# A one-core encoder layer: written order for the mixer's projection units, pooling counts set up later, third T4 ahead and weights three ahead in the up projection

## The chip, the cores and the metric

One of the eight cores of a Trainium2 chip runs the whole program in one launch. The metric is the device time of an execution in microseconds (us). TensorE (PE) multiplies matrices, VectorE (DVE) and ScalarE (ACT) work on tiles of 128 partitions, GpSimd (POOL) does small element-wise work and issues some DMAs, SyncE (SP) issues most of the others.

## The reference

One layer over 2048 tokens of 1024 channels, all in float32:

```python
xn = rmsnorm(x, norm1_g)
u_pool, zq, zf, zi, zo, zg = split(xn @ w_in)
gates = sigmoid(zg + b_gate)
ya = pool_mixer(u_pool, pool_w, pool_scale) @ w_pa    # trailing means, windows 2/4/8/16
yb = hgrn2_mixer(zq, zf, zi, zo, lb, hgrn_norm_g) @ w_pb   # gated linear recurrence, 4 heads
x = x + (gates[0] * ya + gates[1] * yb) @ w_o
h = rmsnorm(x, norm2_g) @ w_up
val, gate = split(causal_depthwise_conv(h, width=3))
x = x + (silu(gate) * val) @ w_down
out = rmsnorm(x, final_g)
```

The pooling branch divides a window sum by a count, min(t, window); the count differs from the window only in the first tokens.

## The kernel before, in words

The 2048 tokens are four blocks of 512. Blocks are taken in pairs, so that the program has two passes, each with a mixer (input projection, pooling, recurrence, the two branch projections, output projection) and a feed-forward part (up projection, convolution and gate, down projection).

The large products use a two-by-two Strassen-like scheme with seven products instead of eight, named P1 to P7. One half of the operands is the pair of token blocks, the other a pair of output or weight quarters. The activations come in seven forms: B11, B21 and B22 are parts of the normalised input, T1 to T4 sums and differences of them (`FORM`). Each form has four tiles (k = 0 to 3). In tile names, x_f0 to x_f3 are B11 and x_f4 to x_f7 are B21 in the mixer; the feed-forward part's begin with m. Each operand is split into a high part, rounded by ACT (a cast), and a low part, the rest, by DVE; a product of one k is three matmuls (high by high, high by low, low by high), so a projection product has twelve.

A unit (`class Unit`) makes two output tiles for both token blocks from the products in the order P1, P6, P5, P7, P2, P4, P3 (`ORDER`). They gather in three PSUM banks: X takes P1 and then P2, Z takes P6, P7 and P4, V takes P5 and P3 (`BANK`). Between them values are taken out: e1 is ACT's copy of X after P1, u2 = e1 - Z after P6 (L1188), u3 = Z - e1 after P7 (L1192), and the four outputs after P2, P7, P4 and P3. So P2 may only write X after e1, P7 only write Z after u2, and P4 only after u3. The mixer has 14 units a pass in the order `PROJ`: fr are the units of the recurrence's forget gates and queries, gr the branch gates, ur the pooling channels. In traces a buffer's number is left out; in listings of an order fr_0 is the first fr unit. The io product (value and output gate of the recurrence, io_X, io_Y, io_Z, io_V) comes ahead of the units and has the same seven products with four banks each.

Weights come through `class Stream`: SP loads a raw tile, ACT and DVE split it (L230, L231) into one of six buffers, and conversion runs at most `LOOKAHEAD` = 4 products ahead of the product being issued. In the io product of the first pass some weights are sums, made by a DMA of POOL that adds to a raw tile (L165); there are eight of these, kept in the list `added`: four for P7's weights and four for P3's. DVE adds others (w8s to w11s, L384).

The code is written as one stream of matmuls (`mm`); every sixth one ticks a list of tasks, which write other engines' work: forms_b_task writes the forms T1 to T4 and B22, setup_task the masks of the recurrence and the reciprocal counts `inv`, hgrn_task the recurrence (its matmuls pl, pk, pv, po, pt stand between the units' on PE). A scheduler then sets the order on each engine by its own estimate of the time: an instruction that it holds to be ready may pass another. `behind(a, b)` forbids that for a and b: a stands behind b. In the up projection the second matmul of each product already stands behind the last matmul of the product before; in the mixer's units nothing holds the products in their order.

setup_task starts with P7 of io. Before, it begins with an iota on POOL, four minima with the windows on POOL (L611) and a reciprocal on DVE (L613), then eight masks and two more, in two scratch tiles in turn. The form T4 in the up projection is B21 - T2 on DVE (L861) and a split. Of its four tiles the third and fourth wait until the first u3 of a unit is written, and stand behind it.

Of the kernel before, what the change touches and what calls it, by code (L numbers as in the profile page):

```python
# [15 lines left out]
ALU = mybir.AluOpType  # L16
# [59 lines left out]
N_OPS = 6  # L76
# [5 lines left out]
def tile_trunk(  # L82
# [85 lines left out]
    class Stream:  # L168
        def __init__(self):
            self.raws = []  # L170
            self.ops = []
            self.n_raw = 0
            self.tiles = []
            self.next = 0
            self.done = 0
            self.pins = {}
            self.stop = None

        def raw(self, src, plus=None):
            r = Raw(src, plus)  # L180
# [57 lines left out]
        def advance(self, n):  # L238
            for _ in range(n):
                j = len(self.tiles)  # L240
                if j >= len(self.ops) or j == self.stop or j >= self.next + LOOKAHEAD or j - N_OPS >= self.done:
                    return
                self.convert()

# [13 lines left out]
    def behind(ins, other):  # L258

        tc.add_manual_dep(ins.ins, other.ins.name, mybir.DependencyInfo(  # L260
            mybir.DependencyClass.NoSync, mybir.DependencyReason.DATA), reason="behind")
# [338 lines left out]
    def setup_task():  # L600
        scratch = [hist.rearrange("p a b -> p (a b)")[:, :64], uhist.rearrange("p a b -> p (a b)")]

        def mask_of():
            scratch.reverse()
            return scratch[0]

        ins = pool.iota(inv[:, 3], pattern=[[1, 16]], base=1, channel_multiplier=0,
                  allow_small_or_imprecise_dtypes=True)
        behind(ins, last_root[0])
        for g, w in enumerate(WINDOWS):  # L610
            pool.tensor_scalar(inv[:, g], inv[:, 3], float(w), None, ALU.min)  # L611
        flat_inv = inv.rearrange("p a b -> p (a b)")
        dve.reciprocal(flat_inv, flat_inv)  # L613
        yield 1
        keys = [(h, h, 0, h) for h in (1, 2, 4, 16)]
        keys += [(8 * h + t, 2 * h, t * h, h) for h in (4, 16) for t in range(2)]
        for key, x, off, w in keys:
            nb = 64 // x
            mf = mask_of()
            behind(pool.memset(mf, 1.0), ins if len(masks) < 6 else added[3])  # L620
            v = mf.rearrange("p (b h) -> p b h", h=x)
            pool.affine_select(out=v, in_=v, pattern=[[-2 * x, nb], [0, x]],
                               compare_op=ALU.is_ge, fill=0.0, base=-off, channel_multiplier=1)
            pool.affine_select(out=v, in_=v, pattern=[[2 * x, nb], [0, x]],
                               compare_op=ALU.is_ge, fill=0.0, base=off + w - 1,
                               channel_multiplier=-1)
            m8 = const.tile([P, 64], U8, tag=f"m{key}", name=f"m{key}")
            yield 2
            pool.tensor_copy(m8, mf)
            masks[key] = m8.rearrange("p (b h) -> p b h", h=x)  # L630
        for t in range(2):
            mf = mask_of()
            behind(pool.memset(mf, 0.0), added[3])
            pool.affine_select(out=mf, in_=mf, compare_op=ALU.not_equal, fill=1.0, base=-t,
                               pattern=[[-2, 64]], channel_multiplier=1)
            m8 = const.tile([P, 64], U8, tag=f"md{t}", name=f"md{t}")
            yield 2
            pool.tensor_copy(m8, mf)
            masks[-1 - t] = m8.unsqueeze(1)
        pool.memset(hist, 0.0)  # L640
        pool.memset(uhist, 0.0)
        for h in range(HEADS):
            pool.memset(state[h, 0], 0.0)

# [146 lines left out]
    def forms_b_task(src, gain, forms, full, after, go, early):  # L791
# [24 lines left out]
        for k in range(4):  # L816
            while len(full["B11"]) <= k:
                yield 4
            p12 = turned(k)
            p22 = turned(k + 4)  # L820
            t = slot(f"{name}b{k}")
            act.activation(t, p22, AF.Copy, scale=negs[:, gain + k + 4 : gain + k + 5])
            b22.append(t)
            t1.append(minus("t1", k, p12, full["B11"][k]))
            t2 = minus("t2", k, p22, t1[k], k + 4)
            if src[0] == "m":
                t = slot(f"{name}t3{k}")
                pool.tensor_tensor(t, full["B11"][k], t2, ALU.subtract)
                t3.append(t)
            elif not early:  # L830
                t3.append(minus("t3", k, p12, b22[k], op=ALU.add))
            forms["T2"].append(split(t2, f"{name}T2{k}"))
            full["T2"].append(t2)
            yield 1
        for k in range(4):
            forms["T1"].append(split(t1[k], f"{name}T1{k}"))
            yield 2 if src[0] == "m" else 5
# [17 lines left out]
        for k in range(4):  # L855
            while len(full["B21"]) <= k:
                yield 4
            t4 = slot(f"{name}t4{k}")
            while src[0] == "m" and k > 1 and not forms.get("u3"):
                yield 1  # L860
            ins = dve.tensor_tensor(t4, full["B21"][k], full["T2"][k], ALU.subtract)  # L861
            if src[0] == "m" and k > 1:
                behind(ins, forms["u3"][0])
            while early and k and len(forms.get("u3", ())) < 4:
                yield 1
            if early and k > 1:
                behind(ins, forms["u3"][3])
            forms["T4"].append(split(t4, f"{name}T4{k}"))
            if early and k == 1:
                behind(last_split[0][1], forms["u3"][3])  # L870
            if early and k:
                stream.pins[20 + k] = last_split[0]
                while len(stream.tiles) <= 20 + k:
                    stream.convert()
                stream.stop = 21 + k if k < 3 else 25
                forms["low"] = stream.low
            if src[0] == "x" and not early:
                forms["B22"].append(split(b22[k], f"{name}B22{k}"))
            yield 1
        while len(forms["B22"]) < 4:  # L880
# [4 lines left out]
            if early:  # L885
# [7 lines left out]
                            stream.convert()  # L893
                stream.stop = 26 + k if k < 2 else None
            yield 1

    x2d = {}

# [254 lines left out]
    class Unit:  # L1153
# [10 lines left out]
        def multiply(self, p, forms, late):  # L1164
# [8 lines left out]
            for k in range(4):  # L1173
                wh, wl = w[:, 0, k * P : (k + 1) * P], w[:, 1, k * P : (k + 1) * P]
                xh, xl = xs[k]
                mm(ps, wh, xh, start=p in FIRST and k == 0, stop=False, skip_group_check=True)
                if k == 0 and self.key == "up":
                    behind(count[1], before)
                mm(ps, wh, xl, start=False, stop=False, skip_group_check=True)
                mm(ps, wl, xh, start=False, stop=k == 3, skip_group_check=True)  # L1180
# [687 lines left out]
```

## Time and profile before

| | |
|---|---|
| median of 3 runs | 2548.97 us |
| lowest and highest | 2546.82 and 2556.62 us |
| profiled execution | 2549.41 us, its span 2547.7 us |
| mean granted PE clock | 0.997 |
| first mixer with its start | 0 to about 640 us |
| first feed-forward part | about 640 to 1275 us |
| second mixer, second feed-forward part | about 1275 to 1890 us, 1890 us to the end |

A timeline row gives the start and the length in us, the engine, the line, the operation, the tile written and those read, sizes, count, and in brackets the idle time ahead of it with what ended it. A row of a window gives the busy time of each engine with the number of instructions, then the PE clock (1.00 is full), the share of DMA engines in use and GB/s. PE's ends are modelled.

### The profile page before, as it was taken

Reading aid. Unit: us, or ns where it says so; the run is one execution under the profiler, and the core shown is the slowest. Engines: PE = TensorE matmul, PEld = TensorE weight load, DVE = VectorE, ACT = ScalarE, POOL = GpSimd, SP = SyncE. Lnnn points to the kernel's source line nnn. Section 1 sums busy time; section 2 is a strip of 40 time slices with the busy share of each in tenths; the row PEclk is TensorE's granted clock in tenths of the full one; section 3 lists DMA queues with packets and bytes.
Section 4 is the critical chain, followed back from the end, with each engine's and each line's share of the span. In section 5 each row is a group of like instructions: output and inputs, shape, how many; then the busy total and the mean of one; then the engine's idle time right before and its main releaser. Section 6 shows DMA issues by size and latency. Waiting matters only on the chain.

```text
span 2547.7 us, 35661 instructions
## 1 busy us (share of the span) xinstructions
PE 2515.0 (99%) x11508; PEld 2059.6 (81%) x11508; DVE 1972.7 (77%) x3508; ACT 1175.5 (46%) x2218; POOL 746.7 (29%) x1127
## 2 busy tenths in 40 slices
PE   8999999999999999999999999999999999999998
PEld 7787877888788888888887888888887888888887
DVE  7799868498899787885586777675979988778755
ACT  5434434334545454554554343442355554545534
POOL 4244353002344334461230111200033433325410
PEclk9999999999999999999999999999999999999999
DMA  8777767777788879997344343446443444446952
GB/s 265 250 188 229 219 184 229 232 220 238 203 239 241 227 227 246 262 362 246 133 145 149 99 133 112 137 153 218 150 158 96 158 151 144 148 140 234 329 163 98
DMA packets 252332, 493.76 MB, mean 194 GB/s; under 512 B 26544, under 2 KB 43056, under 8 KB 251824
## 3 DMA queue, kind: packets, MB, share of 16 engines
q1 hardware_dynamic: 184512, 313.60, 38.2%
q0 software_dynamic: 42656, 112.74, 17.2%
q10 hardware_dynamic: 24976, 65.13, 7.4%
q8 instruction: 91, 1.49, 0.2%
q14 instruction: 97, 0.79, 0.1%
HBM read 381.79 MB, written 187.17 MB: 223 GB/s over the span
## 4 chain that ended last, share of the span: by engine, by line
PE 90%; DVE 5%; DMA 2%; ACT 1%; POOL 1%; issue 1%; SPq 0%; ACTq 0%; POOLq 0%; DVEq 0%
PE dn_P L148 16%; PE up_Z L148 14%; PE up_X L148 10%; PE up_V L148 9%; PE wo_P L148 6%; PE gr_Z L148 4%; PE pa L148 4%; PE pb L148 3%; PE gr_V L148 3%; PE io_Z L148 3%; PE gr_X L148 3%; PE fr_Z L148 2%; PE io_V L148 2%; PE fr_X L148 2%; PE ur_Z L148 1%; PE pl L1018 1%
## 5 line engine op out<-in xcount | busy, mean ns | idle before, releaser
L230 ACT CAST ops<-raw 128x512 fp32r<-128x512 f32 x744 | 459.4, 620 | 832.0 <-PE dn_P L148 176.2
L231 DVE TENSOR_TENSOR ops<-raw,ops 128x512 fp32r<-128x512 f32 x744 | 549.4, 742 | 208.9 <-ACT ops L230 200.8
L1604 DVE SCALAR_TENSOR_TENSOR e<-h,cols,e 128x512 f32<-128x512 f32 x176 | 143.8, 819 | 31.2 <-ACT e L1602 25.8
L1602 ACT ACTIVATE e<-h,cols 128x512 f32<-128x512 f32 x176 | 142.6, 814 | 25.3 <-DVE h L1151 18.4
L1607 DVE SCALAR_TENSOR_TENSOR e<-h,cols,e 128x512 f32<-128x512 f32 x176 | 134.0, 770 | 2.7
L953 POOL DMA_DIRECT2D g_P<-dg_P x154 | 83.7, 545 | 161.4 <-PE dn_P L148 114.4
L1261 POOL TENSOR_TENSOR gf_P<-e,e 128x512 f32<-128x512 f32 x44 | 61.1, 1391 | 149.1 <-DVE e L1613 95.6
L1261 POOL TENSOR_TENSOR gf_P<-gf_P,e 128x512 f32<-128x512 f32 x44 | 59.1, 1344 | 71.8 <-DVE e L1613 71.4
L1399 POOL TENSOR_TENSOR q<-q,qs 128x512 f32<-128x512 f32 x16 | 21.9, 1367 | 198.3 <-ACT qs L1398 191.0
L1597 POOL COPY h<-h 128x2 f32<-128x2 f32 x88 | 40.2, 467 | 131.5 <-DVE h L1150 127.6
L1611 ACT ACTIVATE e<-e 128x512 f32<-128x512 f32 x88 | 55.5, 631 | 40.8 <-DVE e L1607 40.6
L1599 POOL COPY hist<-h 128x2 f32<-128x2 f32 x88 | 37.3, 424 | 116.3 <-DVE h L1151 114.6
L1436 ACT ACTIVATE gt<-gt,cols 128x512 f32<-128x512 f32 x48 | 34.8, 725 | 75.8 <-DVE gt L1151 47.9
L1151 DVE TENSOR_TENSOR h<-up_u,up_V 128x512 f32<-128x512 f32 x88 | 60.2, 684 | 10.7 <-PE up_V L148 10.3
L1236 DVE TENSOR_TENSOR x<-x,wo_P 128x512 f32<-128x512 f32 x88 | 56.3, 691 | 12.1 <-PE wo_P L148 11.9
L1236 DVE TENSOR_TENSOR ac<-ac,dn_P 128x512 f32<-128x512 f32 x72 | 47.2, 683 | 16.7 <-PE dn_P L148 16.5
L1627 POOL DMA_DIRECT2D dg_P<-gf_P x88 | 50.6, 575 | 8.2 <-POOL gf_P L1261 7.4
L1003 POOL COPY qm<-q 128x64 f32<-128x64 f32 x64 | 22.3, 364 | 104.4 <-DVE q L1009 33.3
L1186 ACT COPY up_e<-up_X 128x512 f32<-128x512 f32 x44 | 25.8, 586 | 57.1 <-PE up_X L148 49.9
L1018 PE MATMUL pl<-qm,k 128*128 128x192 f32 x256 | 50.3, 326 | 0.3 <-DVE qm L1007 0.3
L1597 POOL COPY h<-hist 128x2 f32<-128x2 f32 x88 | 44.2, 510 | 20.6 <-issue 20.6
L1018 PEld LDWEIGHTS pl<-qm,k 128*128 128x128 f32 x256 | 44.3, 189 | 4.9 <-issue 0.5
(1285 smaller groups left out, 8108.7 us busy)
## 6 DMA issues: line engine op xcount, KB each, us to landing
g_P<-dg_P POOLq DMA_DIRECT2D x154, 256.0 KB, 6.1
raw<-in_w_up_t SPq DMA_DIRECT2D x132, 256.0 KB, 3.1
raw<-in_w_in_t SPq DMA_DIRECT2D x98, 256.0 KB, 3.2
dg_P<-gf_P POOLq DMA_DIRECT2D x88, 256.0 KB, 3.9
dg_P<-e SPq DMA_DIRECT2D x66, 256.0 KB, 3.7
raw<-in_w_dn SPq DMA_DIRECT2D x66, 256.0 KB, 3.9
x<-in_x SPq DMA_DIRECT2D x64, 256.0 KB, 4.7
gd<-gt ACTq DMA_DIRECT2D x64, 256.0 KB, 3.3
```

What stands on the lines that cost most here:

```text
L148: count[1] = pe.matmul(*args, **kw)
L230: self.mark = act.copy(hi, v)
L231: low = self.low = dve.tensor_tensor(lo, v, f32(hi), ALU.subtract)
L953: eng.dma_start(t, d)
L1018: ins = pe.matmul(pa_[:, c * 192 : c * 192 + 192], ks[:, (i + c) * P : (i + c + 1) * P], mv[:, c].rearrange("p s x -> p (s x)"), start=Tru ...
L1151: return dve.tensor_tensor(dst, t, ps, ALU.add if how == "add" else ALU.subtract)
L1236: dve.tensor_tensor(t, t, ps[j], ALU.add if sg > 0 else ALU.subtract)
L1261: pin(eng.tensor_tensor(t, x0, x1, op))
L1597: pool.tensor_copy(h[:, 0:2], hist[:, mt] if hf == 0 else hs[s, 0][:, TB : TB + 2])
L1602: in_turn(act.activation(t, h[:, 2:], AF.Identity, bias=col(o_cb + mt), scale=col(o_cw + 4 * MF + mt)))
L1604: in_turn(second(dve.scalar_tensor_tensor(t, h[:, 1 : 1 + TB], col(o_cw + 2 * MF + mt), t, ALU.mult, ALU.add)))
L1607: dve.scalar_tensor_tensor(t, h[:, 0:TB], col(o_cw + mt), t, ALU.mult, ALU.add)
```

## The change

Four edits. The second matmul of each product stands behind the last matmul of the product before in all units, not only in those of the up projection. The iota, the minima and the reciprocal go from the front of setup_task to its end, and the iota stands behind the eighth of the adding DMAs; the masks' first memset stands behind the row norm (`last_root`) in its place. In the up projection the third T4 subtraction is no longer behind u3; the DVE half of its split is. And from the splits of T1 to the end of B22 there, conversion runs three products ahead instead of four.

```diff
+            self.room = LOOKAHEAD
...
-                if j >= len(self.ops) or j == self.stop or j >= self.next + LOOKAHEAD or j - N_OPS >= self.done:
+                if j >= len(self.ops) or j == self.stop or j >= self.next + self.room or j - N_OPS >= self.done:
...
-        ins = pool.iota(inv[:, 3], pattern=[[1, 16]], base=1, channel_multiplier=0,
-                  allow_small_or_imprecise_dtypes=True)
-        behind(ins, last_root[0])
-        for g, w in enumerate(WINDOWS):
-            pool.tensor_scalar(inv[:, g], inv[:, 3], float(w), None, ALU.min)
-        flat_inv = inv.rearrange("p a b -> p (a b)")
-        dve.reciprocal(flat_inv, flat_inv)
-        yield 1
...
-            behind(pool.memset(mf, 1.0), ins if len(masks) < 6 else added[3])
+            behind(pool.memset(mf, 1.0), last_root[0] if len(masks) < 6 else added[3])
...
+        while len(added) < 8:
+            yield 1
+        ins = pool.iota(inv[:, 3], pattern=[[1, 16]], base=1, channel_multiplier=0,
+                        allow_small_or_imprecise_dtypes=True)
+        behind(ins, added[7])
+        for g, w in enumerate(WINDOWS):
+            pool.tensor_scalar(inv[:, g], inv[:, 3], float(w), None, ALU.min)
+        flat_inv = inv.rearrange("p a b -> p (a b)")
+        dve.reciprocal(flat_inv, flat_inv)
...
+        if src[0] == "m":
+            stream.room = LOOKAHEAD - 1
...
-            while src[0] == "m" and k > 1 and not forms.get("u3"):
+            while src[0] == "m" and k > 2 and not forms.get("u3"):
+                yield 1
+            ins = dve.tensor_tensor(t4, full["B21"][k], full["T2"][k], ALU.subtract)
+            if src[0] == "m" and k > 2:
+                behind(ins, forms["u3"][0])
+            while src[0] == "m" and k > 1 and not forms.get("u3"):
                 yield 1
-            ins = dve.tensor_tensor(t4, full["B21"][k], full["T2"][k], ALU.subtract)
-            if src[0] == "m" and k > 1:
-                behind(ins, forms["u3"][0])
...
+            if src[0] == "m" and k == 2:
+                behind(last_split[0][1], forms["u3"][0])
...
+        stream.room = LOOKAHEAD
...
-                if k == 0 and self.key == "up":
+                if k == 0:
                     behind(count[1], before)
```

What the scheduler makes of it is seen on PE, at the end of P7 in the first unit of the first mixer (T3 is P7's form, f4 to f7 are P2's, T4 is P4's; gr_0 is the next unit). Before:

```order
L148 MATMUL fr_0_Z<-x_T33h,ops_1254 128x512
L148 MATMUL fr_0_X<-x_f7h,ops_1284 128x512
L148 MATMUL gr_0_X<-x_f0h,ops_1348 128x512
L148 MATMUL gr_0_X<-x_f0l,ops_1348 128x512
...
L148 MATMUL gr_0_X<-x_f3h,ops_1348 128x512
L148 MATMUL fr_0_Z<-x_T40h,ops_1307 128x512
```

After:

```order
L148 MATMUL fr_0_Z<-x_T33h,ops_1254 128x512
L148 MATMUL fr_0_X<-x_f4h,ops_1284 128x512
L148 MATMUL fr_0_X<-x_f4l,ops_1284 128x512
...
L148 MATMUL fr_0_X<-x_f7h,ops_1284 128x512
L148 MATMUL fr_0_Z<-x_T40h,ops_1307 128x512
```

Eleven of P2's matmuls stood ahead of P7 and the twelve of the next unit's P1 ahead of P4; now P2 stands between P7 and P4, and the next unit begins behind P3.

On DVE, at the sums of io's weights in the start (w8s, w9s), before:

```order
L384 TENSOR_TENSOR w8s_488<-w8s_485,raw_322 128x512
L384 TENSOR_TENSOR w9s_502<-raw_353,raw_386 128x512
L613 RECIPROCAL inv<-inv 128x64
L384 TENSOR_TENSOR w9s_505<-w9s_502,raw_419 128x512
L811 SCALAR_TENSOR_TENSOR x_t_541<-x_t_529,cols,x_b_267 128x512
```

After, on DVE at the end of io's P7 (io_u_0 to io_u_3 are its four u3):

```order
L865 TENSOR_TENSOR x_t_924<-x_b_364,x_t_563 128x512
L1316 TENSOR_TENSOR io_u_0_967<-io_Z_701,io_e_0_459 128x512
L643 RECIPROCAL inv<-inv 128x64
L1316 TENSOR_TENSOR io_u_1_977<-io_Z_702,io_e_1_469 128x512
L1316 TENSOR_TENSOR io_u_2_982<-io_Z_703,io_e_2_474 128x512
```

The reciprocal moved from between two sums to between the first and the second u3.

On DVE at P7 of the first unit of the up projection (m_t ahead of m_T42l is the third T4, up_0_u is u3), before:

```order
L657 TENSOR_TENSOR m_T41l<-m_t_6891,m_T41h 128x512
L1192 TENSOR_TENSOR up_0_u_6915<-up_0_Z,up_0_e_6548 128x512
L231 TENSOR_TENSOR ops_6957<-raw_6750,ops_6957 128x512
L1151 TENSOR_TENSOR h_0_1_1_6917<-up_0_u_6915,up_0_V 128x512
L861 TENSOR_TENSOR m_t_6908<-m_b_6448,m_t_6680 128x512
L231 TENSOR_TENSOR ops_6990<-raw_6773,ops_6990 128x512
L657 TENSOR_TENSOR m_T42l<-m_t_6908,m_T42h 128x512
```

After:

```order
L659 TENSOR_TENSOR m_T41l<-m_t_6886,m_T41h 128x512
L865 TENSOR_TENSOR m_t_6903<-m_b_6448,m_t_6680 128x512
L1201 TENSOR_TENSOR up_0_u_6911<-up_0_Z,up_0_e_6548 128x512
L232 TENSOR_TENSOR ops_6985<-raw_6768,ops_6985 128x512
L1160 TENSOR_TENSOR h_0_1_1_6913<-up_0_u_6911,up_0_V 128x512
L659 TENSOR_TENSOR m_T42l<-m_t_6903,m_T42h 128x512
```

The third T4 subtraction now stands ahead of u3, and its split ahead of a weight's low part.

## The prediction

> **What bounds the kernel now.** I read the page's busy line and chain first, then the list of waits of TensorE (PE), then busy time in narrow windows, then the timelines of single places.
>
> ```profile
> PE 2515.0 (99%) x11508; PEld 2059.6 (81%) x11508; DVE 1972.7 (77%) x3508; ACT 1175.5 (46%) x2218; POOL 746.7 (29%) x1127
> PE 90%; DVE 5%; DMA 2%; ACT 1%; POOL 1%; issue 1%; SPq 0%; ACTq 0%; POOLq 0%; DVEq 0%
> ```
>
> PE is busy 2515.0 of 2547.7 us and carries 90% of the chain. No matmul is added or removed, so the time can move only where PE waits or runs at a lower clock. The waits that this change can touch (columns: us in total, times, longest):
>
> ```profile
> PE pl L1058 <- DVE q L977: 5.2, 3, 2.3
> PE io_Z L148 <- ACT ops L230: 2.3, 1, 2.3
> PE gr_X L148 <- ACT gr_e L1186: 2.2, 2, 1.6
> PE gr_Z L148 <- DVE gr_u L1192: 1.5, 2, 1.3
> PE up_Z L148 <- ACT m_T43h L656: 1.1, 2, 0.6
> PE up_Z L148 <- DVE m_T42l L657: 0.6, 2, 0.3
> PE up_Z L148 <- DVE m_T43l L657: 0.5, 2, 0.2
> ```
>
> Together 13.4 us. Windows show what some of them cost beyond the wait (columns: PE, weight loads, DVE, ACT, POOL busy and counts, PE clock, DMA share, GB/s):
>
> ```profile
> 720.00:1072.00 352.00, 352.00 (x1523) 286.14 (x1523) 291.54 (x410) 179.28 (x281) 143.97 (x216) 1.00 0.86 240
> 200.00:300.00 100.00, 97.81 (x503) 81.07 (x502) 86.12 (x202) 43.28 (x106) 38.41 (x43) 1.00 0.79 223
> 125.02:128.43 3.41, 1.73 (x12) 1.33 (x11) 3.41 (x9) 1.07 (x3) 0.10 (x1) 1.00 1.05 384
> 387.84:391.25 3.41, 1.33 (x11) 1.33 (x12) 3.41 (x5) 2.22 (x5) 2.79 (x2) 1.00 0.94 329
> 391.25:394.67 3.42, 3.42 (x14) 2.94 (x13) 3.42 (x9) 1.90 (x4) 1.73 (x2) 0.50 1.00 162
> 677.97:681.39 3.42, 2.31 (x7) 0.97 (x6) 2.68 (x5) 1.36 (x3) 0.00 (x0) 1.00 0.80 229
> 681.39:684.80 3.41, 3.41 (x9) 2.48 (x8) 3.38 (x7) 2.36 (x4) 0.00 (x0) 0.50 0.11 12
> 1394.77:1398.19 3.42, 1.14 (x9) 0.98 (x9) 3.42 (x9) 2.88 (x7) 0.00 (x0) 1.00 0.74 214
> 1398.19:1401.60 3.41, 3.41 (x8) 2.77 (x9) 3.41 (x11) 0.00 (x0) 0.06 (x1) 0.50 0.23 76
> 1934.08:1937.50 3.42, 2.72 (x10) 1.43 (x9) 1.95 (x4) 1.64 (x3) 0.10 (x1) 1.00 0.39 138
> ```
>
> With nothing in its way PE takes 352.00/1523 = 0.231 us a matmul. After three thin stretches of 3.41 us the next 3.41 us run at half clock; each such stretch does half its work, so it costs 3.41/2 = 1.7 us. The two in the mixers follow the pl waits, the one at 681.39 the waits for T42 and T43. Two similar waits, at 125 and at 1934 us, were not followed by one, so the rule is not sharp in these rows.
>
> The Trainium skill, page "TensorE: Matmul & The Clock Gate", section "HAM oscillation — how this bites in real kernels", says as an abstract rule that only PE gaps beyond about 3.4 us bite. This trace does not agree: the idle part of the stretch at 387.84 is 3.41 - 1.33 = 2.08 us, and the clock halved.
>
> **The start: counts later.** POOL's iota and four minima and DVE's reciprocal leave the front.
>
> ```profile
> 34.92 0.55 DVE L613 RECIPROCAL inv<-inv 128x64 f32<-128x64 f32 x1 [1.93 <-POOL inv L611]
> 43.64 0.74 DVE L811 SCALAR_TENSOR_TENSOR x_t<-x_t,cols,x_b 128x512 f32<-128x512 f32 x1
> 44.52 0.70 PE L148 MATMUL io_Z<-ops,x_T20h 128*128 128x512 f32 x2 [2.30 <-ACT ops L230]
> ```
>
> DVE loses 1.93 + 0.47 (the next begins at 35.39) = 2.40 us to the reciprocal, and its queue from there leads to the L811 step that ends at 43.64 + 0.74 = 44.38. It reads the last bank that io_Z needs, and PE starts io_Z at 44.52; the list names ACT, whose cast ends at the same time. All of DVE's queue behind the reciprocal can move up by 2.4 us, PE is free from 44.52 - 2.30 = 42.2, so the 2.30 us wait goes: **-2.3 us** (bounds -2.3 and 0, if one of the weight loads is late instead; I take the first because DVE's idle in these rows is POOL's).
>
> The reciprocal returns between the first and the second of the four u3 subtractions of the io product P7. It then waits for POOL, whose iota and minima stand behind the last accumulating DMA.
>
> ```profile
> 29.99 0.45 POOL L607 IOTA inv<- 128x16 f32 x1
> 30.55 2.86 POOL L611 TENSOR_SCALAR inv<-inv 128x16 f32<-128x16 f32 x3
> 34.64 0.24 POOL L611 TENSOR_SCALAR inv<-inv 128x16 f32<-128x16 f32 x1
> 77.23 1.75 POOL L165 DMA_DIRECT2D raw<-in_w_io  x2 [5.07 <-DMA raw<-kw2ioP]
> 76.75 2.48 DVE L1307 TENSOR_TENSOR io_u<-io_Z,io_e 128x512 f32<-128x512 f32 x4 [3.02 <-PE io_Z L148]
> 78.64 0.63 PE L148 MATMUL io_Z<-ops,x_T40h 128*128 128x512 f32 x2
> ```
>
> The second of the two DMAs is issued about half of 1.75 us behind the first, and POOL is free at 78.5 to 79.0. Iota 0.45 and four minima at 0.24 (the price while DVE stood still, as it will here) make 1.4, so the counts are ready near 80.1; the reciprocal's 0.55 brings the second u3 to 80.7 and its end to 81.35. PE wants it at 78.64: **+2.7 us**. Bounds: 0 if the scheduler's place turns out late enough, +5.5 if the minima take 2.86/3 = 0.95 us each (2.8 more). What is queued behind the reciprocal on DVE (three u3, then the T4 splits) is late by about as much as PE, so nothing more is lost. All these times move up with the start by the 2.3 us, which changes no difference. On POOL the masks now stand ahead of the first accumulating DMAs instead of partly behind, and the five operations taken out there (0.45 + 2.86 + 0.24 = 3.55 us) make room for them; I charge nothing, and 3.55 us of a later DMA would be the most.
>
> **Written order in the mixer.** Before, the scheduler put most of a unit's P2 ahead of P7, and the next unit's P1 ahead of P4. So units fr, whose last product feeds the recurrence, ended a product (12 x 0.231 = 2.8 us) later than they need, and PE then reached the recurrence's pl matmuls too early. Now fr_0 and fr_3 end 2.8 us earlier in the first mixer, fr_0 by 5.1 in the second (22 matmuls), and pl stays where it was: each of the three pl waits (at most 2.3) is smaller than that, so 5.2 us go, and the two half-clock stretches behind them, 2 x 1.7 = 3.4. P2 now stands behind P7, so it waits no longer for the ACT copy of the bank (gr_X, 2.2) and covers u3 before P4 (gr_Z, 1.5). Gain 5.2 + 3.4 + 2.2 + 1.5 = **-12.3 us** (bounds -12.3 and 0).
>
> Against it: P7 needs u2 from DVE, and only P5 is left to cover that. In the first mixer DVE is at 86% (row 200 to 300), and u2 comes late. First, worst and last of seven units in which it will be late:
>
> ```profile
> 158.83 0.68 DVE L1188 TENSOR_TENSOR ur_u<-ur_e,ur_Z 128x512 f32<-128x512 f32 x1
> 159.91 0.39 PE L148 MATMUL ur_Z<-x_T30h,ops 128*128 128x512 f32 x1
> 213.04 0.69 DVE L1188 TENSOR_TENSOR gr_u<-gr_e,gr_Z 128x512 f32<-128x512 f32 x1
> 213.78 0.50 PE L148 MATMUL gr_Z<-x_T30h,ops 128*128 128x512 f32 x1
> 421.06 0.69 DVE L1188 TENSOR_TENSOR gr_u<-gr_e,gr_Z 128x512 f32<-128x512 f32 x1
> 424.90 0.53 PE L148 MATMUL gr_Z<-x_T30h,ops 128*128 128x512 f32 x1
> ```
>
> For each unit I take P7's start less the matmuls that now stand behind it, and compare it with the end of u2, corrected by what moved ahead of it on DVE. For gr_1: u2 ends at 213.73, 0.3 earlier by DVE's order; P7 comes at 213.78 - 2.8 = 210.98; late by 2.4. For ur_0: 159.51 + 0.2 against 159.91 - 1.5, late by 1.3. For gr_6: 421.75 + 1.0 against 424.90 - 2.6, late by 0.4. The same for fr_1 0.6, gr_2 0.9, ur_1 0.5, fr_3 2.3: in all **+8.4 us**. The other seven units, and thirteen of fourteen in the second mixer, have u2 done in time. Bounds: 0 if DVE gets ahead as fr ends earlier, and +24.6 if DVE sets the pace everywhere (all matmuls that moved behind P7 in the first mixer, 106 x 0.231). I take 8.4, which is read from these places themselves. The recurrence's other matmuls (pt, pv, po) also stand up to 2.8 us earlier among PE's; none of them is in the list of waits for more than 1.6 us in all, and I charge nothing for them.
>
> **Up projection.** Twice, at the first two units' P4.
>
> ```profile
> 674.21 0.69 DVE L1192 TENSOR_TENSOR up_u<-up_Z,up_e 128x512 f32<-128x512 f32 x1 [0.82 <-PE up_Z L148]
> 676.11 0.69 DVE L861 TENSOR_TENSOR m_t<-m_b,m_t 128x512 f32<-128x512 f32 x1
> 677.58 0.62 ACT L656 CAST m_T42h<-m_t 128x512 fp32r<-128x512 f32 x1
> 676.81 0.40 PE L148 MATMUL up_Z<-m_T40h,ops 128*128 128x512 f32 x1
> 681.86 0.63 PE L148 MATMUL up_Z<-m_T40h,ops 128*128 128x512 f32 x1
> 685.99 0.39 PE L148 MATMUL up_V<-m_B220h,ops 128*128 128x512 f32 x1
> ```
>
> The third T4 subtraction goes from 676.11 to ahead of u3, into DVE's 0.82 us of idle, which hides its 0.69; with weights three ahead its ACT cast also goes ahead of the weight cast that waited for PE. T42 is then ready before 676.81, T43 some 2 us sooner, by about 679, when PE asks for it. The 24 matmuls of the two P4 take 685.99 - 676.81 = 9.18 us, against 24 x 0.231 = 5.54: 3.6 lost, of which 1.7 is clock. The second pass has the same three waits without the half clock, 1.9. **-5.5 us** (bounds -5.5 and 0). The split's DVE half now stands behind u3, as the subtraction did, and PE asks for it 7 matmuls into P4, so that added order costs nothing. Weights three ahead takes away one converted weight of reserve; the weight cast that now follows T42's still ends before PE's next product asks for it, since three are ready. If the reserve were needed, a product would wait for a cast and a subtraction, 0.62 + 0.69 = 1.3 us each time. B22's splits keep their places, and so does the wait for the last of them.
>
> **New half-clock stretches.** The new waits at gr_1, fr_3 and io's P4 are 2.3 to 2.7 us. Of the five thin stretches shown three were followed by half a clock and two were not, and a wait is often cut by the border of two stretches; I charge one: **+1.7 us** (0 to 5.1). By the 3.4 us of the Trainium skill's page none would be, and the sum would be 1.7 lower.
>
> **Sum.** -2.3 + 2.7 - 12.3 + 8.4 - 5.5 + 1.7 = -7.3 us. The profiled execution took 2549.41 us, 0.4 above the median of 2548.97, so 2549.4 - 7.3 = 2542.
>
> **Rivals.**
> - DVE sets the pace of the first mixer. For it: 86% there. Against it: seven of fourteen units have u2 in time. From the point where u2 comes as late as P7 moved up, the +8.4 becomes +24.6, and three more half clocks 5.1: 2542 + 16.2 + 5.1 = 2563, slower. Chance 0.05; halfway to it (2550) 0.20.
> - DVE moves up with PE, since it waits for PE at fr's ends: no u2 waits and no half clock, 2542 - 8.4 - 1.7 = 2532. Chance 0.14.
> - The start only trades its wait, or loses 2.7 more through slow minima, the rest as summed: 2545. Chance 0.08.
> - The waits are as summed, but no new one is followed by half a clock: 2542 - 1.7 = 2540. For it: the stretches at 125 and 1934. Against it: three rows show the clock halving. Chance 0.13. The rule of the Trainium skill's page on the clock gate, named above, gives this case.
>
> My forecast, 2542, keeps 0.40.
>
> **Range and chances.** 0.5% is 12.7 us, about what a measurement of this kernel can tell from no change. The range 2533 to 2553 holds the forecast and the mild cases, and leaves out the first rival's far end and about half of the second. Faster by over 0.5% means under 2536.2: most of the second rival, 0.12. Slower means over 2561.7: part of the first, 0.03. Within: 0.85.
>
> **What would show it.** Right: the io_Z wait at 44 is gone and one of 2 to 3 us stands at P4's second matmul, with DVE's reciprocal as its releaser; the pl waits and the half-clock rows near 391 and 1398 are gone; short waits of P7 for u L1188 appear in ur_0, gr_1 and fr_3; T42 and T43 leave the list. Wrong: pl waits remain although fr ends sooner (then DVE, not PE's order, sets them), or waits for u L1188 total over 15 us.

## The result and the profile after

| | before | after |
|---|---|---|
| median | 2549.61 us (16 runs, 2545.92 to 2557.08) | 2543.57 us (16 runs, 2540.2 to 2546.4) |
| profiled execution, its span | 2549.41, 2547.7 us | 2540.99, 2539.3 us |
| mean granted PE clock | 0.997 | 0.998 |

The ratio of after to before is 0.9972, 95% interval 0.9964 to 0.998: a gain of 0.28%, inside the bound of 0.5% that the prediction calls no change. Forecast were 2542 us in 2533 to 2553.

The profile after, its busy line and its chain:

```profile
PE 2511.9 (99%) x11508; PEld 2054.1 (81%) x11508; DVE 1979.2 (78%) x3508; ACT 1176.5 (46%) x2218; POOL 752.6 (30%) x1127
PE 90%; DVE 6%; issue 1%; DMA 1%; ACT 1%; POOL 0%; SPq 0%; DVEq 0%; POOLq 0%; ACTq 0%
```

PE has the same 11508 matmuls and still bounds the kernel. The list of PE's waits after (us in total, times, longest), without three that no edit aims at (x_t for x_xs 3.8, pt for ot 1.8, warm for ident 1.4; before 3.5, 1.6 and 1.4):

```profile
PE pl L1027 <- DVE k L1048: 3.6, 2, 1.9
PE io_Z L148 <- DVE io_u L1316: 3.0, 1, 3.0
PE up_V L148 <- DVE m_B223l L659: 1.8, 2, 0.9
PE gr_Z L148 <- DVE gr_u L1197: 1.0, 1, 1.0
PE ur_Z L148 <- DVE ur_u L1197: 0.9, 1, 0.9
PE io_Z L148 <- ACT ops L231: 0.6, 1, 0.6
PE gr_Z L148 <- DVE gr_u L1201: 0.6, 2, 0.4
PE fr_Z L148 <- DVE fr_u L1197: 0.3, 1, 0.3
```

Gone are pl for q (5.2), gr_X for gr_e (2.2) and those for T42 and T43 (2.2), and also one that the prediction doesn't list, pm (the mixing of the pooled channels) for ACT's pl_2h (1.2). The start's io_Z wait fell from 2.30 to 0.6. New are 3.0 at io's P4 and 2.2 for u2 (L1197). pl for k was 1.5 before and is 3.6, at other places (159 and 417 us) than the waits for q.

P4 of io in the timeline after:

```profile
76.68 0.53 POOL L637 IOTA inv<- 128x16 f32 x1
77.29 1.24 POOL L641 TENSOR_SCALAR inv<-inv 128x16 f32<-128x16 f32 x4
78.56 0.55 DVE L643 RECIPROCAL inv<-inv 128x64 f32<-128x64 f32 x1 [3.23 <-POOL inv L641]
79.03 1.82 DVE L1316 TENSOR_TENSOR io_u<-io_Z,io_e 128x512 f32<-128x512 f32 x3
79.71 1.22 PE L148 MATMUL io_Z<-ops,x_T40h 128*128 128x512 f32 x2 [3.01 <-DVE io_u L1316]
```

DVE stands 3.23 us in front of the reciprocal for POOL's minima, the second u3 comes behind it, and PE waits 3.01 us. Windows there (columns as in the prediction):

```profile
76.29:79.70 3.41, 0.41 (x2) 0.00 (x0) 1.14 (x3) 0.00 (x0) 1.94 (x6) 1.00 0.85 128
79.70:83.12 3.42, 3.41 (x8) 2.76 (x9) 3.33 (x6) 1.03 (x2) 0.00 (x0) 0.50 0.17 31
```

This is the only half-clock stretch after, apart from the end of the kernel. Those at 391, 681 and 1398 us are not there.

How far the same matmul of the program moved against the profiled run of before, in us (minus is sooner), for after and for four of the experiments below:

| first matmul of | before at | after | order alone | counts alone | up alone | reciprocal moved |
|---|---|---|---|---|---|---|
| io | 14.46 | -0.44 | -0.12 | -0.09 | +0.28 | -0.05 |
| io's Z | 44.52 | -2.09 | -0.11 | -1.76 | +0.29 | -1.72 |
| the units, first mixer | 100.21 | +2.75 | -0.12 | +4.89 | +0.29 | -1.71 |
| pb, first mixer | 508.07 | -1.42 | -4.15 | +5.68 | -1.46 | -4.57 |
| up, first pass | 634.31 | -1.64 | -4.39 | +5.64 | -1.49 | -4.61 |
| down, first pass | 1064.36 | -4.17 | -5.66 | +2.81 | -4.22 | -7.85 |
| the units, second mixer | 1369.08 | -3.86 | -4.84 | +3.11 | -3.71 | -7.24 |
| pb, second mixer | 1765.54 | -7.90 | -8.87 | +3.92 | -5.22 | -11.18 |
| up, second pass | 1891.69 | -7.97 | -9.03 | +3.63 | -5.23 | -11.38 |
| down, second pass | 2320.23 | -8.93 | -9.67 | +5.70 | -6.93 | -12.65 |
| last matmul | 2539.13 | -8.62 | -9.29 | +5.81 | -6.95 | -12.28 |

After, io's Z gains 1.65 (2.09 less the 0.44 by which the run started sooner); from there to the units 4.84 are lost; the first mixer gains 4.17, the second 4.04; the up projections gain 2.53 and 0.96.

Each column compares one execution with one. How far that can lead astray is shown by the run below with the third T4 alone: its mixers have PE's matmuls in the same order as before, and yet its first mixer came out 2.93 us shorter and its second 1.50. The clock was not halved there in that execution, neither near 391 nor near 1398 us.

### The profile page after: what moved, and what is told of

Its sections match the earlier page's. It is cut to its first block, busy times and chain, and to the rows that moved or that the text cites. A ratio compares the mean times of both kernels' runs of the same rounds, so it can differ in the third digit from the quotient of the medians.

```text
span 2539.3 us, 35647 instructions
## 1 busy us (share of the span) xinstructions
PE 2511.9 (99%) x11508; PEld 2054.1 (81%) x11508; DVE 1979.2 (78%) x3508; ACT 1176.5 (46%) x2218; POOL 752.6 (30%) x1127
## 3 DMA queue, kind: packets, MB, share of 16 engines
q8 instruction: 91, 1.49, 0.3%
## 4 chain that ended last, share of the span: by engine, by line
PE 90%; DVE 6%; issue 1%; DMA 1%; ACT 1%; POOL 0%; SPq 0%; DVEq 0%; POOLq 0%; ACTq 0%
PE dn_P L148 16%; PE up_Z L148 14%; PE up_X L148 10%; PE up_V L148 9%; PE wo_P L148 6%; PE gr_Z L148 4%; PE pb L148 4%; PE pa L148 3%; PE gr_X L148 3%; PE gr_V L148 3%; PE fr_Z L148 2%; PE io_Z L148 2%; PE fr_X L148 2%; PE fr_V L148 2%; PE io_V L148 1%
## 5 line engine op out<-in xcount | busy, mean ns | idle before, releaser
L1408 POOL TENSOR_TENSOR q<-q,qs 128x512 f32<-128x512 f32 x16 | 21.7, 1358 | 187.4 <-ACT qs L1407 180.8
```

## The experiments

### The parts of the change alone

The written order alone is the last line of the diff, `if k == 0:`, in the kernel before.

> The kernel before with the written order of products alone. Theory A (the terms of the change stand beside each other, each worth what the two traces show in its stretch of the program): first mixer 4.2 us shorter and second mixer 4 to 5 us shorter, the waits of pl on q and the half-clock stretches near 391 and 1398 us gone, some 2 us of waits for u2 in the first mixer instead; the kernel some 8 us shorter, so 0.997 of before. The front stays as before (the wait of 2.3 us at io_Z near 44 us is there) and so do the 24 products of the up projection. Theory B (the mixer gained from work that the other two parts moved, and a half-clock stretch only falls elsewhere): the mixers gain under 4 us together, the kernel is within 3 us of before.

Measured: 2542.27 us, ratio 0.9974 (0.9964 to 0.9983). The table shows 4.03 us in each mixer, as after. PE's waits that bear on it:

```profile
PE io_Z L148 <- ACT ops L230: 2.3, 1, 2.3
PE ur_Z L148 <- DVE ur_u L1188: 1.5, 1, 1.5
PE pl L1018 <- POOL u L917: 1.5, 1, 1.5
PE pl L1018 <- DVE k L1039: 1.4, 1, 1.4
```

No pl waits for q, and u2 is waited for 2.0 us in all (beside the 1.5, rows of 0.3 and 0.2). The pl matmuls wait 3.9 us for other things (beside the two rows, 1.0 for qm), where it was 1.8 before. Theory A holds: the written order's gain doesn't need the other edits.

The later counts alone move iota, minima and reciprocal to the end of setup_task, as in the diff.

> The kernel before with the pooling counts later, alone. Theory A (the front gives 2.1 us, the reciprocal between the first and the second u3 of io costs the wait of 3.0 us at the second product of P4, and that thin stretch brings the half clock of 3.4 us near 80 us, worth 1.7 us): the kernel some 2 to 3 us longer than before, with that wait and that stretch in its trace. Theory B (the half clock near 80 us is chance and not due to the wait): the wait of 3.0 us is there with the clock full behind it, and the kernel within 1 us of before.

Measured: 2548.6 us, ratio 1.0002 (0.9993 to 1.0011), no change. In the profiled run the wait at P4 was 4.1 us, and two half-clock stretches followed it (windows of that run):

```profile
75.84:79.26 3.42, 1.24 (x6) 0.65 (x4) 0.00 (x0) 0.00 (x0) 2.38 (x5) 1.00 0.61 155
79.26:82.67 3.41, 1.53 (x4) 1.24 (x5) 2.68 (x5) 0.00 (x0) 0.55 (x3) 0.50 0.64 104
82.67:86.09 3.42, 3.42 (x10) 2.65 (x9) 3.31 (x6) 1.68 (x4) 0.00 (x0) 0.50 0.22 67
```

From io's Z to the units it lost 6.65 us, and this execution (2555.24) is the slowest of the eleven: its clock was halved at five more places. The wait and the half clock behind it are there as theory A says, and larger, but the time is as theory B says: the median shows none of the 2 to 3 us. Why is open. The half clocks differ between executions, as the section on the hardware shows, and only this one was profiled.

The two edits of the up projection alone:

> The kernel before with the two edits of the up projection alone. Theory A: 24 products of the first pass in 5.8 us instead of 9.2 (the half clock of 681 us gone with the waits), 2 us less in the second pass, up to half a microsecond of each given back at the wait for B223l: the kernel 4.5 to 5.5 us shorter than before. Theory B (what the up projection gains is given back by the end of the down projection, where the landmarks drift by about a microsecond): 3 us shorter or less.

Measured: 2543.58 us, ratio 0.9985 (0.9976 to 0.9993). The ratio says 3.8 us, the medians 5.4. The table has 2.73 and 1.70 us between up and down. That lies between the two theories: some of what is gained at the P4s is lost again before the down projection, though not as much as B says. After, too, stands 5.11 us ahead right behind the first P4s, 4.66 at the wait for B223l and 4.17 at the down projection.

The three ratios multiply to 0.9961 against 0.9972 for all together; each is uncertain by 0.001, so that is no evidence of more than a sum.

### Which half of the written order carries it

The condition was split: once `if k == 0 and (self.key == "up" or p == "P1"):`, which only keeps the next unit from starting early, and once with `p != "P1"`, which only keeps the order inside a unit.

> The kernel before with half of the written order: the next unit's first product P1 no longer goes ahead of the last products P4 and P3 of the unit before; P2 may still go ahead of P7. Theory A (the recurrence's wait for q is there because TensorE arrives early, and it goes once fr ends 12 products sooner): the pl waits on q (5.2 us in three) fall under 1 us and with them the half clocks near 391 and 1398; gr_X on gr_e (2.2) and gr_Z on gr_u (1.5) stay, no wait for u2 appears; 5 to 8 us shorter than before. Theory B (the gain of the written order comes from P2 behind P7, as cover for u3): the pl waits stay and the time is within 2 us of before.

> The kernel before with the other half of the written order: P2 stays behind P7 within a unit; the next unit's P1 may still go ahead of P4. Theory A: gr_X on gr_e (2.2) and gr_Z on gr_u (1.5) go, short waits of P7 for u2 appear, 2 us in all, fr ends as late as before and the pl waits on q stay near 5.2 us with their half clocks; within 2 us of before. Theory B: the pl waits go here, and this half carries the gain of 7 us that the whole written order alone had.

Measured: 2551.0 us, ratio 1.0007 (0.9998 to 1.0017) for the next unit alone; 2555.32 us, ratio 1.0029 (1.0018 to 1.004) for the order within a unit. Neither half gains, the second loses 0.3%, and both together gain 0.26%. With the next unit alone theory A falls; the waits stay and the time is near the 2 us of theory B, but its reason, that the other half carries the gain, falls with the second run. There both theories fall: gr_X no longer waits and short waits for u2 appear, as A says, but the kernel is 0.3% slower, and B's gain is not there. Both profiled executions are the slowest of their kernels. From PE's waits, of the first and of the second:

```profile
PE pl L1058 <- DVE q L977: 3.7, 2, 3.4
PE pt L1136 <- DVE ot L1130: 3.8, 1, 3.8
```

```profile
PE pl L1058 <- DVE q L977: 8.1, 3, 3.6
```

The chain to q at fr_3 (first mixer) shows why the wait there stayed. In each run: u3 of fr_3, the forget gate's value f from bank V, and the first product L977 that pl waits for. Before:

```profile
374.49 0.69 DVE L1192 TENSOR_TENSOR fr_u<-fr_Z,fr_e 128x512 f32<-128x512 f32 x1 [0.62 <-PE fr_Z L148]
388.27 1.50 DVE L977 TENSOR_TENSOR q<-q,f 128x256 f32<-128x256 f32 x1
```

Next unit only:

```profile
373.14 0.69 DVE L1192 TENSOR_TENSOR fr_u<-fr_Z,fr_e 128x512 f32<-128x512 f32 x1 [1.54 <-PE fr_Z L148]
389.50 0.41 DVE L977 TENSOR_TENSOR q<-q,f 128x256 f32<-128x256 f32 x1
```

Within a unit only:

```profile
382.90 0.69 DVE L1192 TENSOR_TENSOR fr_u<-fr_Z,fr_e 128x512 f32<-128x512 f32 x1 [0.88 <-PE fr_Z L148]
393.79 0.69 DVE L1151 TENSOR_TENSOR f<-fr_u,fr_V 128x512 f32<-128x512 f32 x1 [0.88 <-PE fr_V L148]
397.27 0.41 DVE L977 TENSOR_TENSOR q<-q,f 128x256 f32<-128x256 f32 x1
```

Whole written order:

```profile
367.60 0.69 DVE L1192 TENSOR_TENSOR fr_u<-fr_Z,fr_e 128x512 f32<-128x512 f32 x1
381.37 0.41 DVE L977 TENSOR_TENSOR q<-q,f 128x256 f32<-128x256 f32 x1
```

q follows u3 by 13.8, 16.4, 14.4 and 13.8 us: DVE has that much to do between them, and it begins only when P7 is done. With the next unit held back alone, fr_3's last matmul ends 3.7 us sooner than before (379.6 instead of 383.3). But P2 still stands ahead of P7, u3 begins only 1.35 us sooner, and DVE takes 2.6 us more from there to q: the operations are the same, but single ones are longer (one L965 takes 2.26 us, before 0.54), for which no list gives a reason. So q is ready at 389.9, no sooner than before, and PE, which asks for it 1.0 us sooner (at 386.6), waits longer (3.41 instead of 2.30). With the order inside the unit alone, P7 no longer stands behind P2, but the next unit's twelve matmuls stand ahead of P4; f then waits 0.88 us for bank V, and the chain starts again from there. With the whole order u3 stands 6.9 us sooner than before and q with it, 6.4 of which were gained in the units ahead (u2 of fr_3 at 363.77 instead of 370.19), and PE asks for q only 4.2 us sooner. That both P7 and the end of fr must move up is read from these four chains; no run shows it by itself.

The chain at fr_3 is not all. With the next unit alone, the wait for q at fr_0 did fall, from 1.68 to 0.31, and the one of the second pass went. That run lost its time elsewhere, above all at the wait of pt for ot near 481 us (3.8, before 1.6) with two half-clock stretches behind its start; why ot was late there is open.

### The up projection's two edits apart

Room of three alone, and the third T4 alone, each in the kernel before.

> The kernel before with only the weights three ahead during the splits of m. Theory A (ScalarE's cast of T43 stood behind a weight cast that waited for TensorE): the wait for m_T43h (1.1 us in two) goes, those for m_T42l and m_T43l by VectorE stay (1.1 together); the 24 products of the first P4s take some 6.5 us without a half clock, 8.2 with one. Theory B: the casts are late because the subtraction is, and the wait for m_T43h stays.

> The kernel before with only the third subtraction T4 ahead of u3. Theory A: the waits for m_T42l go (0.6 in two), that for m_T43h stays, since ScalarE's casts still stand behind a weight cast; half of the gain of both edits. Theory B: this edit alone brings the whole gain at the place, 24 products in 5.8 us, and the weights three ahead bring nothing.

Measured: 2549.24 us, ratio 1.0 (0.999 to 1.001) for the room; 2542.85 us, ratio 0.9981 (0.997 to 0.9993) for the T4. With the room alone PE's waits are:

```profile
PE up_Z L148 <- ACT m_T43h L657: 1.1, 2, 0.6
PE up_Z L148 <- DVE m_T42l L658: 0.6, 2, 0.3
PE up_Z L148 <- DVE m_T43l L658: 0.4, 2, 0.2
```

all as before; the 24 matmuls of the first two units' P4 took 7.77 us, in an execution whose clock was not halved there, against 9.18 with the half clock before. With the T4 alone the waits are gone, and the 24 matmuls run from the first to the second of these rows in 5.73 us:

```profile
673.78 0.40 PE L148 MATMUL up_Z<-m_T40h,ops 128*128 128x512 f32 x1
679.51 0.39 PE L148 MATMUL up_V<-m_B220h,ops 128*128 128x512 f32 x1
```

Theory B of both holds: the cast of T43 was late because its subtraction stood in line behind the late third one, and the room adds nothing.

### The reciprocal behind the gate additions

In the changed kernel:

```diff
-        dve.reciprocal(flat_inv, flat_inv)
+        while not gates_io:
+            yield 1
+        behind(dve.reciprocal(flat_inv, flat_inv), gates_io[3])
...
                     behind(forms["gate"][0], forms["low"])
+                    gates_io.extend(forms["gate"])
```

> The changed kernel with one edit more: VectorE's reciprocal of the counts stands behind the last of the four gate additions of io, so that it no longer stands between the first and the second u3. Theory A: the wait of 3.0 us at P4's second product near 79 us and the half clock behind it both go: 4.7 us less than the changed kernel (2539), and the start keeps its 2.1 us. Theory B (the half clock at 80 us doesn't hang on the wait): 3 us less, the stretch is still there. Rival C (the reciprocal held back makes the first pooling product late, since the scale by the counts waits for it): part of the gain comes back as a wait in io's end or at fr's first unit.

Measured: 2535.95 us, ratio to the kernel before 0.9952 (0.994 to 0.9964), and so better than both. The four u3 stand together again, and the second product of P4 follows the first:

```profile
75.02 2.48 DVE L1319 TENSOR_TENSOR io_u<-io_Z,io_e 128x512 f32<-128x512 f32 x4 [2.04 <-PE io_Z L148]
76.68 0.39 PE L148 MATMUL io_Z<-ops,x_T40l 128*128 128x512 f32 x1
76.91 0.63 PE L148 MATMUL io_Z<-ops,x_T40h 128*128 128x512 f32 x2
```

From io's Z to the units nothing is lost now (-1.72 and -1.71 in the table), where the changed kernel lost 4.84: theory A. Nothing came back later, so rival C falls.

The same kernel with the weights four ahead throughout:

> The changed kernel with the reciprocal behind the gate additions, but weights four ahead throughout, as before the change. Theory A (the third T4 carries the whole gain of the up projection, the room nothing): within 1.5 us of the kernel with the reciprocal moved (2536), T42 and T43 not in the list of waits. Theory B (both are needed once the order is written): the waits for T43 return, 1 to 2 us more.

Measured: 2534.87 us, ratio to the kernel before 0.9939 (0.9924 to 0.9954). T42 and T43 are not in its list of waits. The room can be left out here too.

### Does the wait make the half clock?

The changed kernel, with the first product's three matmuls of P4 repeated n times on PE while it would stand still:

```diff
+                    if (p, k, j, b0) == ("P4", 0, 0, 0):
+                        for _ in range(n):
+                            xh, xl = xs[0]
+                            pe.matmul(bk[kb][0], xh[:, :P], w[:, 0], start=False, stop=False, skip_group_check=True)
...
```

> The changed kernel, with the three matmuls of the first product of P4 in io repeated twice (six matmuls more, which TensorE runs while it would wait for the second u3; the gate of the first rows is then not the reference's). The u3 still comes when it comes, so 1.4 of the 3.0 us of waiting become work and nothing is won by that alone. Theory A (a grid stretch of 3.41 us in which TensorE stands still for over about 2.0 us makes the next one run at half clock): the idle part falls to 1.6 us, no half clock follows near 80 us, and fr's first product starts 1.7 us sooner than in the changed kernel (near 101.3 where the start is the same), the wait in the list about 1.6 us. Theory B (the half clock has another cause, the load of new weights or a transfer): it is still there behind the shorter wait, and fr starts at 103.

Measured, with n = 2: the counts came later on POOL in this run, the second u3 with them, and 2.50 us of waiting were left instead of 1.6. So it didn't tell the theories apart:

```profile
77.40:80.82 3.42, 0.92 (x5) 0.43 (x4) 1.58 (x3) 0.00 (x0) 1.50 (x6) 1.00 0.86 142
80.82:84.23 3.41, 3.41 (x10) 2.63 (x9) 3.33 (x7) 1.14 (x2) 0.00 (x0) 0.50 0.07 11
```

> As the kernel with six matmuls more, but with fifteen (the three of the first product of P4 five times more; the gate of the first rows is not the reference's). With six, the second u3 came 0.7 us later than in the changed kernel, 2.50 us of the wait were left, all of them in one grid stretch (0.92 of 3.41 us busy), and the next stretch ran at half clock. Fifteen take 3.5 us, from 76.3 to 79.8, and the second u3 ends between 79.7 and 80.4. Theory A (standing still for over about 2.0 us of a grid stretch halves the next): 0.1 to 0.6 us of wait is left, no half clock near 80, and fr's first product starts 1.0 to 1.7 us sooner than with six, although nine more matmuls run (101.9 to 102.6 instead of 103.6). Theory B (another cause at this place, which the matmuls don't remove): the half clock stays, fr at 103.6 or later.

Measured, with n = 5:

```profile
79.03:82.44 3.41, 3.41 (x16) 2.63 (x14) 0.93 (x2) 0.00 (x0) 2.15 (x7) 1.00 0.77 117
82.44:85.85 3.41, 3.41 (x15) 2.56 (x15) 3.32 (x7) 0.81 (x2) 0.00 (x0) 1.00 0.21 37
```

PE is busy and the clock stays full. This run began later (its io's Z stood at +0.36), so the expected absolute times don't apply: fr's first product started at 104.4, but only 59.5 us behind io's Z, against 61.4 with n = 2. From P4's second product to the first product of the units it took 21.7 us, against 23.2 both in the changed kernel and with n = 2: 1.5 us less for the same work, as theory A says. That is what the half clock cost at this place, 1.7 by the prediction. The medians, 2542.1 and 2541.04 us, lie 1.5 and 2.5 under the changed kernel's, though matmuls were added; differences of this size can't be told between the launches.

## Why the prediction was right, and where it was not

The time came out 1.6 us from the forecast, and the kernel moved 6 us in the medians and 8.4 in the profiled runs, against 7.3. That it came so close is partly luck, for errors made up for each other: by the table the mixers gained 4.3 us more than their two terms say (8.2 instead of 3.9), the up projections gained 2.0 less, the start 0.65 less, and P4 of io lost 0.4 more.

- **Start, -2.3.** Right in kind: io_Z's wait fell from 2.30 to 0.64 us, and io's Z gained 1.65. The rest is still the wait for ACT's cast.
- **Reciprocal at P4, +2.7, and new half clock, +1.7.** Right: 3.01 us of wait, releaser and place as named, and one half-clock stretch, together 4.84 us where 4.4 was forecast. The counts came at 78.5, where 80.1 less the start's gain was forecast.
- **Written order, -12.3.** The waits went as listed: pl for q, gr_X, two half clocks, and 0.9 of gr_Z's 1.5. Not foreseen were 2.1 us more of pl for k, and that the 1.2 of pm for pl_2h would go. The two half clocks are not a steady gain of the order: with the T4 alone the pl waits for q stood as before (2.30 us at 388.62), and the clock stayed full. The reason given, that fr ends 2.8 us sooner while pl stays, held at fr_0 but is half of it at fr_3: with the next unit held back alone, fr_3 ended 3.7 us sooner, but P7's u3 moved up by 1.35 only, and pl waited longer. What also had to move, by the chains above, was P7, ahead of P2.
- **u2 late, +8.4.** This term was mis-sized: it measured 2.2 us in the list, in three units (ur_1 0.90, fr_3 0.27, gr_5 0.97), of which gr_5 was held to be in time. Rows of timelines show that u2 does release P7 in seven units, as many as forecast (P7 starts 0.05 us behind its end, with gr_3 and gr_5 in the place of ur_0 and fr_1), but counted from PE's starts they cost only 3.0 us together. (The term's upper bound, 106 x 0.231, is 24.5 and not 24.6; nothing hangs on it.) The step behind the term took DVE's times from the trace before, corrected only by DVE's own order. But DVE had been waiting for PE there, above all at the u3 that P7 now releases sooner. From the list of DVE's waits, before:

```profile
DVE fr_u L1192 <- PE fr_Z L148: 15.1, 5, 6.2
DVE gr_u L1192 <- PE gr_Z L148: 7.8, 5, 2.5
```

and after:

```profile
DVE fr_u L1201 <- PE fr_Z L148: 7.3, 4, 3.6
DVE gr_u L1201 <- PE gr_Z L148: 3.2, 4, 1.1
```

These are both passes: 12.4 us less, of which 5.7 in the first mixer, to which the term belongs. For gr_1 a wait of 2.4 was forecast. Ahead of it DVE's longest idle, in front of u3 of fr_0, fell from 6.16 us (first row, before) to 3.60 (second row, after):

```profile
114.09 0.69 DVE L1192 TENSOR_TENSOR fr_u<-fr_Z,fr_e 128x512 f32<-128x512 f32 x1 [6.16 <-PE fr_Z L148]
114.27 0.69 DVE L1201 TENSOR_TENSOR fr_u<-fr_Z,fr_e 128x512 f32<-128x512 f32 x1 [3.60 <-PE fr_Z L148]
```

The next one, in front of fr_0's q, fell from 2.06 to 0.57 (PE too), and 3.50 us in front of fr_1's f, for which the list names ACT, went. So u2 of gr_1 stood at 211.14 instead of 213.04, although the units began 2.75 us later, and P7 began when it was done, with no wait in the list (0.1 us by PE's starts):

```profile
211.14 0.68 DVE L1197 TENSOR_TENSOR gr_u<-gr_e,gr_Z 128x512 f32<-128x512 f32 x1
211.87 0.50 PE L148 MATMUL gr_Z<-x_T30h,ops 128*128 128x512 f32 x1
```

That is the second rival (DVE moves up with PE, chance 0.14) for most of this term, so -12.3 + 8.4 = -3.9 was -8.2 in the two mixers (4.17 and 4.04): by the list, -12.3 + 2.2 + 2.1 + 0.6 (the rest of gr_Z) - 1.2 (pm) = -8.6.
- **Up projection, -5.5.** Right at the place and too large in all. The P4s did what was said: 24 matmuls in 5.75 us instead of 9.18, and in 5.74 instead of 7.75 in the second pass, together 5.4. At the down projections 2.53 and 0.96 of it, 3.5 us, were left: the wait for B223l behind the P4s rose from 1.3 to 1.8, and half a microsecond to one more was lost over the rest of each pass, for which no wait is listed. And 1.4 of the 5.4 is the clock: with the written order alone the same waits were there, the clock was not halved near 681 us, and the first 24 matmuls took 7.75 us. The room, to which the sooner T43 was put down, gave nothing; the third T4 gave it all.
- **Rival without a new half clock, 2540.** After the 3.01 us wait the clock did halve, so this rival fell. The rule of the Trainium skill's page on the clock gate, which the prediction names for it, does not hold at this place.

## What to carry to other kernels

When a product is moved ahead of others, the engine that waits for it can move up too: before charging a new wait to that engine, look in its own list of waits for how long it stands for the product that is moved. Two halves of an edit can gain nothing apart and yet gain together, as the two halves of the written order did here, so try them together before one is thrown out. An instruction that waits for a slow engine, put between short ones in a queue, cost the wait and a stretch of half clock here; placed a few instructions further behind, it cost nothing.

## What was not expected of the hardware

The half clock looked like a rule that is not sharp. It is nearly sharp if the stretches are cut on the grid on which the clock changes in that launch (3.413 us, and its start differs from launch to launch), and PE's idle time is counted from the starts of its matmuls (the distance to the next one, less the median distance of that shape). In the thirteen profiled executions, between 20 and 2500 us, 26 stretches at full clock were idle for 2.03 us or more, and 25 of them were followed by one at half clock (the other was idle for 2.10); of 41 that were idle for 1.5 to 2.02 us, one was (2.01). These counts shift by one or two with the way in which the median is taken. The busy column of the windows hides this: the stretch ahead of 681 us before shows 2.31 us busy of 3.42, yet was idle for 2.03 by starts, since the row of a matmul lasts 0.39 us where the next one starts 0.23 us behind it.

So whether a wait of about 2 us costs up to 1.7 us more depends on where the launch's grid cuts it. The same wait for ot near 466 us, with the written order alone and then with the reciprocal moved:

```profile
466.54:469.95 3.41, 1.68 (x8) 1.03 (x6) 1.51 (x4) 1.73 (x3) 0.00 (x0) 1.00 1.05 265
```

```profile
465.06:468.47 3.41, 1.58 (x9) 0.97 (x7) 2.01 (x6) 1.73 (x3) 0.00 (x0) 1.00 1.08 276
468.47:471.88 3.41, 3.41 (x10) 2.67 (x9) 2.10 (x5) 0.00 (x0) 0.00 (x0) 0.50 1.09 279
```

The first is idle for 1.90 us, its wait ends 0.10 us behind the border, and the next stretch runs at full clock; the second is idle for 2.08 us, its wait lies within the stretch, and the clock halves. The Trainium skill, page "TensorE: Matmul & The Clock Gate", section "What's actually happening", says that the activity window is 3413 ns long and runs freely. The grid in these traces agrees. The 3.4 us of idle time that the same page names there, and in the section that the prediction quotes, do not: 2.03 us in one window were enough.

The spread between executions of one kernel goes with the clock too. Of thirty of the kernel before, ten with a granted clock of 0.996 took 2551.4 us in the mean, eight with 0.997 took 2548.6, nine with 0.998 took 2547.4, two with 0.999 took 2545.2. One half-clock stretch is 3.41 x 0.5 / 2548 = 0.0007 of the mean clock, so 0.003 are four to five stretches, 7 to 8 us, and the means differ by 6.2. A profiled run alone, like that of the counts alone with eight of them behind its start, can be off by more than the change is worth. What is left open is the slow loss of 0.5 to 1 us along each pass of the feed-forward part against the kernel before, which no wait in the lists names.
